# Four products of two heads' weighted sums side by side in a fixed order: the grouped layers of a hybrid decoder trunk

## The chip, the cores and the metric

The kernel runs on one core of one Trainium2 chip. The metric is the device time of one execution in microseconds (us), lower is better. The kernel before takes 2571.69 us, the median of 3 runs between 2570.69 and 2571.88.

## What is computed

The reference is a trunk of four decoder layers for 256 rows of 2048 features in fp32. Layers 0 and 3 are latent attention, layer 1 is sparse attention with a top-k selection, layer 2 is attention in a window of 128 keys. Every layer also has four heads that attend to a memory, a gate over all head outputs, and an output projection. Layers 1 and 2 have 32 query heads of 64 features that share 4 key and value heads. The part that the change touches is the last line of their attention, the weighted sum of the values. Layer 2, cut to what matters (layer 1 differs in which keys a query may see, and has no sink):

```python
def block(args):
    qb, kb, vb, start = args
    ...
    s = jnp.einsum('bqgjd,bkgd->bgjqk', qb, kb, preferred_element_type=jnp.float32) * scale + bias
    s = jnp.where(valid, s, NEG_INF)
    m = jnp.maximum(jnp.max(s, axis=-1, keepdims=True), sink)
    e = jnp.exp(s - m)
    p = e / (jnp.sum(e, axis=-1, keepdims=True) + jnp.exp(sink - m))
    return jnp.einsum('bgjqk,bkgd->bqgjd', p.astype(vb.dtype), vb)
...
y = jnp.concatenate([self_out, mem_out], axis=-1) * jax.nn.silu(gate)
x = x + y @ w_out[i]
```

## The kernel before

**Projections.** All weights stream from DRAM through one ring of buffers (`wr`). ScalarE copies each piece of 128x512 into a rounded part `wh` (L74), VectorE takes the remainder `wl` (L83), and TensorE multiplies both parts with activations that are split in the same way. `rows_by` (its matmuls are L289) gives rows, `columns_by` (L310 for `wh`, L314 for `wl`) gives columns. These make up most of TensorE's work. `wh` and `wl` have three buffers each, so ScalarE waits where TensorE has not yet let go of one.

**A grouped layer.** `Grouped.project(g)` makes the queries of one key head `g` (eight query heads, as two halves of four), a bias tile and the gate tile `gT`. `Grouped.attend` then goes through the two halves. In each half it treats two sets, `odd` 0 and 1. A set holds two heads, and its 64 queries of one of four quarters stand as 128 columns. For each set `quarter_softmax` goes over the two halves `b` of the rows: score products (`sp`, L1033 and L1036), bias, minimum and exponential on VectorE and ScalarE, division by the sum, and `weights_T`, which transposes the weights on TensorE into a PSUM tile `ptp` (L550), two transposes for `b = 0` and four for `b = 1`. ScalarE copies the result into `pT[odd]` (L1061, recorded under the copy helper's line L74). The text calls the two sets the even and the odd head.

**The sums.** When both sets have their weights, four fp32 matrix products form the tile `o` in one PSUM bank (L1065). `v` is the stationary side, 128 keys by 64 features; the weights `pT` are the moving side. The even set's sums go to the partitions 0 to 63, the odd one's to 64 to 127, by the `tile_position`, which names the half of the array's columns. The first key tile (`t = 0`) streams 512 columns of weights, the second one (`t = 1`) only 256, as the first two quarters of the queries come before all of its keys. In the source the order is even and odd for `t = 0`, then even and odd for `t = 1`. Afterwards VectorE multiplies `o` with the gate (L1070) and the result is split into the two parts of `y`, which the output projection takes (L289, `acc_wo`).

**What sets the order.** The kernel is written for a framework whose planner decides the order of the instructions on each engine: it plays the program through with a model of times, and picks what it takes to be ready. An instruction may thus stand far from its place in the source, as long as what it depends on comes first. Writes to one PSUM tile keep their source order. `keep_in_program_order` pins one instruction: it adds an edge to the instruction that was traced just before it on the same engine, which sets an order of issue and is no wait for an end. It says nothing about what the planner puts between the two. The order of `project`, `attend` and the output projection of the part before (`w_out`) in the source is that of the loop over parts; the planner lets their matmuls run among the score and sum products of `attend`.

Of the kernel before, what the change touches and what calls it, by code (L numbers as in the profile page):

```python
# [16 lines left out]
S = 256  # L17
# [28 lines left out]
def kernel(ctx: ExitStack, tc: tile.TileContext, a: dict, out: bass.AP,  # L46
                             kinds=(0, 1, 2, 0)):
    nc = tc.nc
# [8 lines left out]
    def misc(name, dt=F32):  # L57
        return ps.tile([P, 512], dt, name=name, tag="mp", bufs=4)

    def tmp(name, n=512, dt=F32):  # L60
        return wk.tile([P, n], dt, name=name, tag=f"t{n}", bufs=4)
# [11 lines left out]
    def copy_act(o, i, scale=1.0):  # L73
        inst = nc.scalar.activation(o, i, AF.Copy, scale=scale)  # L74
        if pinned:
            tc.keep_in_program_order(inst)
# [4 lines left out]
    def split(hi, lo, src):  # L81
        copy_act(hi, src)
        nc.vector.tensor_sub(lo, src, f32(hi))  # L83
# [175 lines left out]
    def other_work():  # L259
        for _ in range(2):  # L260
            if steps and next(steps[0], None) is None:
                steps.pop(0)
# [294 lines left out]
    def attend(o, v, pT):  # L557

        for n_, (l, r_) in enumerate(((v[0], pT[0]), (v[0], pT[1]), (v[1], pT[0]))):
            nc.tensor.matmul(o, l, r_, start=n_ == 0, stop=False)  # L560
        nc.tensor.matmul(o[:, P:], v[2], pT[2], start=False, stop=True)
# [24 lines left out]
    def quarter_softmax(score, bias, first_key, both, b, nsk):  # L586

        es = []
        mn, sm = small("mn", 2), small("sm", 2)
        for i, r in enumerate((2 * b, 2 * b + 1)):  # L590
            k0, k1 = first_key(r), (r + 1) * 64
            n = k1 - k0
            sp = score(r, k0, n)
            u = wk.tile([P, S], F32, name="u", tag="e", bufs=4)
            e = wk.tile([P, S], F32, name="e", tag="e", bufs=4) if nsk is None else u
            for z0, z1 in ((0, k0), (k1, (b + 1) * P)):
                if z0 < z1:
                    nc.gpsimd.memset(e[:, z0:z1], 0.0)
            bi, at = bias(r, k0, k1), u[:, k0:k1]
            if both(r):  # L600
                nc.vector.tensor_add(at, sp[:, n:2 * n], bi)
                bi = at
            nc.vector.tensor_tensor_reduce(at, sp[:, :n], bi, -1.0, nsk if nsk is not None else BIG,
                                           op0=OP.add, op1=OP.min, accum_out=mn[:, i:i + 1])
            nc.scalar.activation(e[:, k0:k1], at, AF.Exp, bias=mn[:, i:i + 1], scale=-1.0,
                                 accum_out=sm[:, i:i + 1])
            es.append((e, k0, k1))
        rc = small("rc", 2)
        if nsk is not None:
            d = small("sd", 2)  # L610
            nc.vector.tensor_scalar(d, mn, nsk, None, op0=OP.subtract)
            e2 = small("se", 2)
            nc.scalar.activation(e2, d, AF.Exp)
            s3 = small("sa", 2)
            nc.vector.tensor_add(s3, sm, e2)
            nc.vector.reciprocal(rc, s3)
        else:
            nc.vector.reciprocal(rc, sm)
        for i, (e, k0, k1) in enumerate(es):
            copy_act(e[:, k0:k1], e[:, k0:k1], scale=rc[:, i:i + 1])  # L620
        return weights_T([e for e, _, _ in es], [(i, k) for k in range(b + 1) for i in range(2)])
# [82 lines left out]
    class Latent:  # L704
# [121 lines left out]
        def attend(self, qn, qr, kn, v, gT):  # L826
            y = act.tile([P, 2, 4, S], F32R, name="y", tag="y", bufs=2)
            for h in range(4):
                def score(b):
                    sp = misc("sp")  # L830
                    qs = slice(b * P, (b + 1) * P)
                    q, k, z = qn[h // 2], kn[h // 2], h % 2
                    if b == 0:
                        seq = [(q[:, 0, z, qs], k[:, :, z, :P]), (q[:, 1, z, qs], k[:, :, z, :P]),
                               (qr[:, h, qs], self.kr[:, :, :P])]
                    else:
                        seq = [(q[:, 0, z, qs], k[:, :, z, :]), (q[:, 1, z, qs], k[:, 0, z, :]),
                               (qr[:, h, qs], self.kr)]
                    for n_, (l, r_) in enumerate(seq):
                        n = r_.shape[-1] * (r_.shape[1] if len(r_.shape) == 3 else 1)  # L840
                        nc.tensor.matmul(sp[:, :n], l, r_, start=n_ == 0, stop=n_ == 2)
                    return sp
                tp = masked_softmax(score, lambda b, n: caus[:, S - n:], self.scale)
                pT = wk.tile([P, 768], F32R, name="pT", tag="pT", bufs=PT)
                pT = pT[:, :S], pT[:, S:2 * S], tmp("pf")[:, :P]
                split(pT[0], pT[1], tp[:, :S])
                copy_act(pT[2], tp[:, S:S + P])
                if h % 2 == 0:
                    o = misc("o")
                attend(o[:, (h % 2) * S:(h % 2 + 1) * S],  # L850
                       [z[:, h * P:(h + 1) * P] for z in v], pT)
                if h % 2 == 1:
                    gated(y, o, gT, h - 1)
            return y


    class Grouped:
# [164 lines left out]
        def attend(self, g, q, bm, gT):  # L1022
            while steps:
                other_work()
            y = act.tile([P, 2, 4, S], F32R, name="y", tag="y", bufs=2)
            for half in range(2):
                pT = []
                for odd in range(2):
                    def score(r, k0, n):
                        sp = misc("sp")  # L1030
                        qb = q[half][:, odd, r].rearrange("p j c -> p (j c)")
                        if both(r):
                            nc.tensor.matmul(sp[:, :2 * n], qb, self.k[:, g, :, k0:k0 + n], start=True, stop=True)  # L1033
                        else:
                            for v in range(2):
                                nc.tensor.matmul(sp[:, :n], qb, self.k[:, g, v, k0:k0 + n],  # L1036
                                                 start=v == 0, stop=v == 1)
                        return sp

                    def bias(r, k0, k1):  # L1040
                        c0 = (3 - r) * 64
                        bh = bm[:, half * 2 + odd, c0 + k0:c0 + k1]
                        if not self.sparse or r == 0:
                            return bh
                        bs = wk.tile([P, S], F32, name="bs", tag="e", bufs=4)[:, :k1]
                        nc.vector.tensor_add(bs, bh, self.sel[r])
                        return bs

                    def first_key(r):
                        return 64 if r == 3 and not self.sparse else 0  # L1050

                    def both(r):
                        return r < 3 or not self.sparse

                    u0 = g * 4 + half * 2 + odd
                    nsk = None if self.sparse else nsink[:, u0:u0 + 1]
                    pT.append(wk.tile([P, 6, P], F32, name="pT2", tag="pT", bufs=PT))
                    for b in range(2):
                        tp = quarter_softmax(score, bias, first_key, both, b, nsk)
                        i0, i1 = ((0, 2), (2, 6))[b]  # L1060
                        copy_act(pT[odd][:, i0:i1], tp[:, :(i1 - i0) * P].rearrange("p (i c) -> p i c", c=P))  # L1061
                o = misc("o")
                for t in range(2):
                    for odd in range(2):
                        nc.tensor.matmul(o[64 * odd:64 * odd + 64, t * S:], self.v[:, t, g * 64:g * 64 + 64],  # L1065
                                         pT[odd][:, 4 * t:4 + 2 * t].rearrange("p i c -> p (i c)"),
                                         start=t == 0, stop=t == 1, tile_position=(0, 64 * odd))
                j = half * 2
                yt = tmp("yt")
                nc.vector.tensor_mul(yt.rearrange("p (j r c) -> p j r c", j=2, r=4),  # L1070
                                     o.rearrange("p (r j c) -> p j r c", r=4, j=2),
                                     gT[:, j:j + 2, :].rearrange("p j (r c) -> p j r c", r=4))
                split(y[:, 0, j:j + 2, :], y[:, 1, j:j + 2, :], yt.rearrange("p (a b) -> p a b", a=2))
            return y
# [237 lines left out]
```

## Time and profile before

| what | value |
|---|---|
| median of 3 runs | 2571.69 us (2570.69 to 2571.88) |
| the profiled execution's own time | 2570.63 us |
| its span, first to last instruction | 2568.9 us |
| granted TensorE clock, mean | 0.999 |
| TensorE matmul busy | 2558.5 us |
| VectorE busy | 1885.3 us |
| ScalarE busy | 1596.3 us |
| DMA, mean over the span | 199 GB/s |

A row of the timeline gives the start and the length in us, the engine, the line, the operation, the tile that is written and those that are read, the shapes, and after `x` how many instructions of one kind in succession are merged in the row. PE is TensorE; PEld is its weight load, which can run beside a matmul. A row of the groups gives the count after `x`, then the busy time of all together, the mean length in ns, and the idle time before them. A row of the waits names who waited for whom, then the total in us, how often, and the longest. A matmul's recorded length overlaps with the next ones, so the step from one start to the next says more of its price than its length.

### The profile page before, as it was taken

The page shows a single profiled execution, that of the slowest core. Times are in us where ns is not written, and L with a number is a line of the kernel's source. Part 1 is how long each engine was busy: PE and PEld are TensorE (multiplying, and loading weights), DVE is VectorE, ACT ScalarE, POOL GpSimd, SP SyncE. Part 2 cuts the span into 40 slices and gives each one's busy share as a digit, 9 for nine tenths or more (in the row PEclk, how much of TensorE's full clock was granted, in tenths as well). Part 3 has the DMA queues.
Part 4 walks back from the last instruction along what each step waited for, and adds up shares of the span by engine and source line. Part 5 has one row for each costly group of instructions (what it writes and reads, how often), then busy time and mean ns, then how long its engine had stood idle before and what let it go on. Part 6 is the DMA issues. An engine that isn't in the chain of part 4 may idle for free.

```text
span 2568.9 us, 41673 instructions
## 1 busy us (share of the span) xinstructions
PE 2558.5 (100%) x14022; PEld 2186.3 (85%) x14022; DVE 1885.3 (73%) x3800; ACT 1596.3 (62%) x3271; POOL 102.9 (4%) x297
## 2 busy tenths in 40 slices
PE   9999999999999999999999999999999999999998
PEld 8888898888888889888888888888888888888887
DVE  6666667677777687987777777777768767777766
ACT  6556556566566566666666566666656666666655
POOL 1200000000000000000000000000000000000000
PEclk9999999999999999999999999999999999999999
DMA  9888777576677667665666565565555768666765
GB/s 310 262 265 257 238 224 227 165 196 178 183 203 204 185 199 205 197 194 164 185 181 175 170 214 179 165 180 166 176 168 161 238 189 221 190 195 186 222 168 185
DMA packets 478583, 511.68 MB, mean 199 GB/s; under 512 B 70656, under 2 KB 391040, under 8 KB 477728
## 3 DMA queue, kind: packets, MB, share of 16 engines
q1 hardware_dynamic: 461856, 451.82, 59.9%
q0 software_dynamic: 15792, 56.22, 7.0%
q8 instruction: 110, 1.80, 0.3%
q14 instruction: 105, 0.86, 0.1%
q10 hardware_dynamic: 720, 0.98, 0.1%
HBM read 483.67 MB, written 29.46 MB: 200 GB/s over the span
## 4 chain that ended last, share of the span: by engine, by line
PE 98%; DMA 1%; DVE 1%; ACT 0%; issue 0%; SPq 0%; POOL 0%; ACTq 0%; DVEq 0%
PE acc_wo L289 20%; PE acc_g L310 14%; PE acc_g L314 7%; PE acc_mv L289 7%; PE acc_q L310 5%; PE acc_mk L310 5%; PE acc_mq L310 4%; PE acc_cq L310 3%; PE acc_qn L310 3%; PE acc_q L314 2%; PE acc_mk L314 2%; PE acc_mq L314 2%; PE acc_cq L314 2%; PE acc_qr L310 2%; PE acc_qn L314 2%; PE acc_va L289 2%
## 5 line engine op out<-in xcount | busy, mean ns | idle before, releaser
L83 DVE TENSOR_TENSOR wl<-wr,wh 128x512 fp32r<-128x512 f32 (+1 forms) x1712 | 1154.5, 679 | 581.1 <-ACT wh L74 551.5
L74 ACT ACTIVATE wh<-wr 128x512 fp32r<-128x512 f32 (+1 forms) x1712 | 1063.0, 623 | 830.9 <-PE acc_g L310 148.1
L310 PE MATMUL acc_g<-xT,wh 128*128 128x512 f32 x1536 | 483.4, 397 | 0.0
L289 PE MATMUL acc_wo<-wh,y 128*128 128x512 f32 x1504 | 477.1, 392 | 0.0
L289 PEld LDWEIGHTS acc_wo<-wh,y 128*128 128x128 f32 x1504 | 282.5, 188 | 58.9 <-ACT th L531 1.5
L314 PEld LDWEIGHTS acc_g<-xT,wl 128*128 128x128 f32 x1536 | 280.8, 188 | 60.6 <-DVE wl L83 0.5
L314 PE MATMUL acc_g<-xT,wl 128*128 128x256 f32 x1536 | 306.0, 281 | 0.1
L289 PE MATMUL acc_wo<-wl,y 128*128 128x512 f32 x752 | 297.7, 396 | 0.0
L310 PEld LDWEIGHTS acc_g<-xT,wh 128*128 128x128 f32 x1536 | 235.3, 189 | 0.8
L289 PEld LDWEIGHTS acc_wo<-wl,y 128*128 128x128 f32 x752 | 141.4, 188 | 25.9
L310 PE MATMUL acc_q<-xT,wh 128*128 128x512 f32 x512 | 161.3, 396 | 0.0
L310 PE MATMUL acc_mq<-xT,wh 128*128 128x512 f32 x512 | 161.1, 396 | 0.0
L310 PE MATMUL acc_mk<-mT,wh 128*128 128x512 f32 x512 | 160.7, 395 | 0.0
L289 PE MATMUL acc_mv<-wh,mT 128*128 128x512 f32 x512 | 156.8, 390 | 0.2
L310 PE MATMUL acc_qn<-cT,wh 128*128 128x512 f32 x384 | 121.0, 396 | 0.0
L310 PE MATMUL acc_cq<-xT,wh 128*128 128x512 f32 x384 | 120.9, 396 | 0.0
L1231 DVE TENSOR_TENSOR xc<-xc,acc_wo 128x1024 f32<-128x1024 f32 x92 | 112.0, 1218 | 4.2 <-PE acc_wo L289 3.4
L314 PEld LDWEIGHTS acc_mk<-mT,wl 128*128 128x128 f32 x512 | 95.8, 188 | 22.6 <-DVE wl L83 0.2
L289 PEld LDWEIGHTS acc_mv<-wh,mT 128*128 128x128 f32 x512 | 96.3, 188 | 20.7 <-ACT wh L74 0.9
L314 PEld LDWEIGHTS acc_q<-xT,wl 128*128 128x128 f32 x512 | 95.0, 188 | 21.5
L314 PEld LDWEIGHTS acc_mq<-xT,wl 128*128 128x128 f32 x512 | 94.5, 188 | 21.4 <-issue 0.4
L314 PE MATMUL acc_mq<-xT,wl 128*128 128x256 f32 x512 | 101.8, 280 | 0.0
(325 smaller groups left out, 3837.1 us busy)
## 6 DMA issues: line engine op xcount, KB each, us to landing
wr<-in_w_out_dram SPq DMA_DIRECT2D x188, 512.0 KB, 3.7
wr<-in_w_in_a_dram SPq DMA_DIRECT2D x176, 512.0 KB, 4.2
wr<-in_w_mem_kv_dram SPq DMA_DIRECT2D x126, 512.0 KB, 4.8
wr<-in_w_in_b_dram SPq DMA_DIRECT2D x116, 512.0 KB, 3.6
wr<-in_w_in_c_dram SPq DMA_DIRECT2D x104, 512.0 KB, 3.5
wr<-in_w_uq_dram SPq DMA_DIRECT2D x288, 128.0 KB, 2.8
wr<-in_w_in_a_dram SPq DMA_DIRECT2D x32, 288.0 KB, 3.1
mv<-mv POOLq DMA_DIRECT2D x16, 512.0 KB, 6.5
```

The source lines that it names most:

```text
L74: inst = nc.scalar.activation(o, i, AF.Copy, scale=scale)
L83: nc.vector.tensor_sub(lo, src, f32(hi))
L289: nc.tensor.matmul(acc[t][:, :n], q[:, v, (s + k) % 4, t * P:(t + 1) * P], w_[:, :n], start=s + k == 0 and v == 0 and w_ is wh, stop=s + k ...
L310: nc.tensor.matmul(acc[j], wh[:, o:o + P], q[:, :, kt % 4, :], start=kt == 0, stop=False)
L314: nc.tensor.matmul(acc[j][:, 0, :], wl[:, o:o + P], q[:, 0, kt % 4, :], start=False, stop=kt == kts - 1)
L1231: nc.vector.tensor_add(xs, xs, acc)
```

## The change

The two nested loops keep their products; only the order of the inner loop turns, and each product is pinned behind the matmul that was traced before it. For the first of the four that is the last transpose of the odd set's weights.

```diff
                 o = misc("o")
                 for t in range(2):
-                    for odd in range(2):
-                        nc.tensor.matmul(o[64 * odd:64 * odd + 64, t * S:], self.v[:, t, g * 64:g * 64 + 64],
-                                         pT[odd][:, 4 * t:4 + 2 * t].rearrange("p i c -> p (i c)"),
-                                         start=t == 0, stop=t == 1, tile_position=(0, 64 * odd))
+                    for odd in (1, 0):
+                        tc.keep_in_program_order(
+                            nc.tensor.matmul(o[64 * odd:64 * odd + 64, t * S:], self.v[:, t, g * 64:g * 64 + 64],
+                                             pT[odd][:, 4 * t:4 + 2 * t].rearrange("p i c -> p (i c)"),
+                                             start=t == 0, stop=t == 1, tile_position=(0, 64 * odd)))
```

## The prediction

> **What bounds the kernel now.** I read the page's busy times first, then the chain that ended last, then the waits, and then the timeline of TensorE around the changed line, where every term of the sum comes from.
>
> ```profile
> span 2568.9 us, 41673 instructions
> PE 2558.5 (100%) x14022; PEld 2186.3 (85%) x14022; DVE 1885.3 (73%) x3800; ACT 1596.3 (62%) x3271; POOL 102.9 (4%) x297
> ...
> PE 98%; DMA 1%; DVE 1%; ACT 0%; issue 0%; SPq 0%; POOL 0%; ACTq 0%; DVEq 0%
> ```
>
> TensorE is busy for 2558.5 of 2568.9 us, and 98% of the chain is its own instructions, one behind another. VectorE has a quarter of the span free, ScalarE over a third. The waits say the same from the other side:
>
> ```profile
> PE wu L122 <- DVE ones L116: 1.1, 1, 1.1
> PE msp L663 <- DMA mkr<-mkT: 0.6, 1, 0.6
> ...
> ACT wh L74 <- PE acc_g L310: 148.1, 223, 2.1
> ```
>
> The first two rows are all that TensorE waited for another engine: 1.7 us. The third is ScalarE, which splits the weights, waiting 148.1 us for TensorE to give a weight buffer back. So the makers of the weights stand behind TensorE, and what is taken from TensorE's stream should come off the time. Only the two grouped layers contain the changed line. There are 16 groups of products (2 layers, 4 key heads, 2 halves), and the question is what each group takes out of TensorE's stream. Its row in the groups, and the two shapes kept apart:
>
> ```profile
> L1065 PE MATMUL o<-pT,vs 128*64 128x256 f32 (+1 forms) x128 | 41.2, 505 | 0.0
> ...
> L1065 PE MATMUL o<-pT,vs 128*64 128x512 f32 x64 | 34.3, 618 | 0.0
> L1065 PE MATMUL o<-pT,vs 128*64 128x256 f32 x64 | 19.8, 392 | 0.0
> ```
>
> 64 and 64 for 16 groups: each group has four matrix products, and each product is recorded as two passes. The two products of the first key tile stream 512 columns, those of the second 256 (they skip the queries that this tile cannot reach). The means of 618 and 392 ns can't simply be added, since passes lie beside each other. So I go by the distance from start to start in the timeline. A group of the first half (TensorE only):
>
> ```profile
> 1123.22 0.27 PE L550 MATMUL ptp<-ident,e 128*128 128x128 f32 x1
> 1123.42 1.07 PE L1065 MATMUL o<-pT,vs 128*64 128x512 f32 x2
> 1124.42 0.50 PE L1033 MATMUL sp<-kd,qS 128*128 128x128 f32 x2
> 1124.76 0.49 PE L550 MATMUL ptp<-ident,e 128*128 128x128 f32 x3
> 1125.01 0.36 PE L314 MATMUL acc_g<-xT,wl 128*128 128x256 f32 x1
> ...
> 1128.30 0.39 PE L289 MATMUL acc_wo<-wl,y 128*128 128x512 f32 x1
> 1128.53 0.39 PE L289 MATMUL acc_wo<-wh,y 128*128 128x512 f32 x1
> 1128.84 1.50 PE L1065 MATMUL o<-pT,vs 128*64 128x512 f32 x6
> 1130.28 0.50 PE L289 MATMUL acc_wo<-wh,y 128*128 128x512 f32 x1
> 1130.62 0.40 PE L289 MATMUL acc_wo<-wl,y 128*128 128x512 f32 x1
> ```
>
> and the last group of all, which is of the second half:
>
> ```profile
> 1879.59 0.27 PE L550 MATMUL ptp<-ident,u 128*128 128x128 f32 x1
> 1879.79 1.07 PE L1065 MATMUL o<-pT,vs 128*64 128x512 f32 x2
> 1880.79 0.55 PE L550 MATMUL ptp<-ident,u 128*128 128x128 f32 x3
> 1881.09 0.49 PE L314 MATMUL acc_mq<-xT,wl 128*128 128x256 f32 x2
> ...
> 1885.24 1.50 PE L1065 MATMUL o<-pT,vs 128*64 128x512 f32 x6
> 1886.67 0.39 PE L314 MATMUL acc_mq<-xT,wl 128*128 128x256 f32 x1
> ```
>
> The even head's 512-column product (two passes) runs **alone**, in the middle of the odd head's transposes. The other three products come about 5.4 us later as one block of six passes. All 16 groups have this form, 8 like the first and 8 like the last. The lone product takes 1124.42 - 1123.42 = 1.00 us of TensorE. The block of three products takes 1130.28 - 1128.84 = 1.44 us although it streams twice as many columns (2 x (512 + 256 + 256) against 2 x 512). Inside the block:
>
> ```profile
> 1128.84:1128.85 0.01, 0.01 (x1) 0.01 (x2) 1.00 0.00 0
> 1128.85:1129.11 0.26, 0.26 (x2) 0.19 (x4) 1.00 0.00 0
> ```
>
> These are stretches of that line alone (length, TensorE busy, passes in flight, weight loads busy, clock, DMA). From 1128.85 on two passes are in flight, at most 0.01 us apart, at a clock of 1.00. Two narrow windows of the timeline show single passes later in the block:
>
> ```profile
> 1129.32 0.59 PE L1065 MATMUL o<-pT,vs 128*64 128x512 f32 x1
> ...
> 1129.97 0.38 PE L1065 MATMUL o<-pT,vs 128*64 128x256 f32 x1
> ```
>
> The first is the odd 512-column product's second pass, which starts 0.48 us after its first; the other is the last pass, of the odd 256-column product. The even head's 256-column product, which writes the other 64 partitions of the sum, lies wholly beside the odd head's 512-column one and costs nothing.
>
> **The change, part by part.** No instruction is added or taken away. The source order becomes odd first tile, even first tile, odd second, even second, and each is pinned behind the matmul traced before it. The odd head's first product stands behind that head's last transpose, so the even head's first product, now pinned behind it, can't be issued early any more.
>
> Removed: the lone product from its place. Its price is the sequence with it against the same sequence without it, which the trace has for other heads:
>
> ```profile
> 1087.06 0.60 PE L550 MATMUL ptp<-ident,e 128*128 128x128 f32 x4
> 1087.41 0.48 PE L314 MATMUL acc_q<-xT,wl 128*128 128x256 f32 x2
> ...
> 1110.74 0.27 PE L550 MATMUL ptp<-ident,e 128*128 128x128 f32 x1
> 1110.77 0.48 PE L1033 MATMUL sp<-kd,qS 128*128 128x128 f32 x2
> 1111.09 0.49 PE L550 MATMUL ptp<-ident,e 128*128 128x128 f32 x3
> 1111.34 0.48 PE L314 MATMUL acc_g<-xT,wl 128*128 128x256 f32 x2
> ```
>
> Second half: four transposes up to the next weight matmul take 1087.41 - 1087.06 = 0.35 us. With the product among them they take 1881.09 - 1879.59 = 1.50. The place costs 1.15 us: 1.00 for the product and 0.15 for what the neighbours lose at its edges. First half: transpose, two score products, three transposes take 1111.34 - 1110.74 = 0.60 us, with the product 1125.01 - 1123.22 = 1.79, so 1.19. Over the groups: 8 x 1.15 + 8 x 1.19 = 18.7 us.
>
> Added: the even 512-column product in the block. The trace doesn't show two 512-column products side by side, so it has two bounds. From below it is the stagger, 0.01 us: as in the block of before, the even product lies beside the odd one. The two second-tile products then lie beside each other where the odd one now runs alone, and the block stays at 0.48 + 0.43 + 0.22 + 0.22 + 0.09 = 1.44 us (the steps between the starts above, each pass as long as its columns, and the exit). It could not be less, as the odd head's four passes set it. From above the product is not overlapped at all: two passes, 0.48 + 0.43 = 0.91 us. I take 0.01, because for the 256 columns that overlap in the rows of before the odd product's passes keep exactly the step (0.48) that the lone product's have, so a second stream beside them slowed nothing. For 16 groups: 0.2 us.
>
> The wait. The block waits for ScalarE's copy of the odd head's weights out of PSUM, as its odd product does now:
>
> ```profile
> 1125.29 0.60 ACT L74 ACTIVATE pT<-ptp 128x512 f32<-128x512 f32 x1 [1.93 <-PE ptp L550]
> ```
>
> It ends at 1125.89, 2.95 us before the block starts; this stretch lies behind the lone product and loses no cover with it. Behind the block on TensorE's queue stand the output projection's and the next weight matmuls, and VectorE's gating product (L1070) waits for it, as before. No DMA is issued or moved and SP and POOL are passed by nothing. The PSUM bank of the sums is taken 5.4 us later, which only frees it for the scores. What is late next: the weight splits must come 18.7 us earlier in sum between 1123 and 1887 us, 2%, against a quarter idle on VectorE.
>
> Sum: 18.7 - 0.2 = 18.5 us. The profiled execution took 2570.63 us (1.7 outside its span), 1.06 below the median of 2571.69. 2570.63 - 18.5 = 2552.1, as a median **2553.2 us**. The planner lays out all instructions anew from its own model. I allow 3 us either way for that: a change of shape costs about 0.1 us (1128.53 to 1128.84 is 0.31 us where the step before it is 0.23), and two more or fewer per group make 16 x 0.2.
>
> **A rule that speaks against it.** In the rows above the even head's pass starts by 1128.85, ahead of the odd head's second pass at 1129.32, though its product stands behind the odd one in the source. So passes of the two column halves do not wait for each other's turn there. Were starts to keep the source order, the even first pass would begin at 0.49 in the block and its second at 0.92, the odd second-tile passes at 0.93 and 1.15, and the even ones at 1.35 and 1.57: the block ends at 1.88, 0.44 longer, 7.0 us in all, and the time is 2553.2 + 7.0, about 2560. The Trainium skill, page "TensorE: Matmul & The Clock Gate", Part 3, section "The mechanism", states just this rule: matmuls start and end in program order, strictly first in, first out, while tiles in different positions start about 4 ns apart. The trace agrees with the small stagger and, at the level of passes, not with the strict order.
>
> **The rivals.**
> - *Two pairs instead of four* (other matmuls planned between the first and the second tile's products; a pin holds only the order). The pair of 512 then costs what the lone product costs now (1.17 us, the mean of 1.15 and 1.19). Today's block with its edges takes 0.08 (entry, 0.31 - 0.23) + 1.44 + 0.11 (the 0.34 after it, less 0.23) = 1.63. The pair of 256 takes 0.08 + 0.27 + 0.22 + 0.09 + 0.11 = 0.77, where the 0.27 is a 256-column pass with the 0.05 by which a block's first pass is longer (0.48 against 0.43). A group saves 0.86, together 13.8: 2558. Against it: today's three stand together in the groups shown, though the planner was free to part them.
> - *Strict order*, above: 2560.
> - *No overlap*: 16 x (1.17 - 0.91) = 4.2 us saved, 2567.5.
> - *The cover goes* (slower). The planner could set the block right behind the transposes, since it counts four products there. TensorE then stands from 1125.01 to the copy's end at 1125.89, 0.9 us, and that nearly eats the 1.17: 2567. If a weight split (0.6 us on ScalarE, as the copy) goes ahead of the copy, it stands 1.5 us and the kernel becomes slower by 16 x 0.33 = 5.3 us, 2577. It decides from a wait of 1.17 us on. Against it: the block's start has 2.95 us of cover, and the planner knows the wait.
> - *Nothing comes off*, because another engine sets the pace: 2571.7. Against it speaks ScalarE's wait for TensorE.
>
> **How the numbers follow.** A measurement of this kernel can tell about 0.2%, 5.1 us, from no change. The forecast has 0.77, two pairs 0.07, strict order 0.06, no overlap 0.02, the cover gone without loss 0.03, with loss 0.03, another pace 0.02. Faster by over 0.2% (below 2566.5): 0.77 + 0.07 + 0.06 = 0.90. Within: 0.02 + 0.03 + 0.02 = 0.07. Slower: 0.03. The range takes the forecast with its 3 us and reaches to the strict order with some: 2549.5 to 2562.
>
> **What would show it.** Right: no `o<-pT,vs` row of two passes alone; 16 blocks of eight passes, each about 1.44 us from its start to the next matmul, with two 512-column passes in flight from the first 0.01 us; odd transposes that again take 0.35 us or 0.60 to the next weight matmul; the busy time of L1065 down from 41.2 us (its row in the groups) to about 25; no new TensorE wait. Wrong: a block near 1.9 or 2.3 us (order or no overlap), or idle TensorE ahead of L1065 released by the copy `pT<-ptp`. The forecast falls if L1065 shrinks as said and the span does not.

## The result, and the profile after

The changed kernel takes 2555.85 us (median of 6 runs, 2554.03 to 2556.82), the kernel before 2571.28 in the same runs (6 runs, 2570.51 to 2571.88). The ratio is 0.994 with a 95% interval of 0.9927 to 0.9952. That is 15.4 us faster, where the forecast was 18.5 (2553.2). The profiled execution took 2556.82 us.

The page of the kernel after, its first lines and the chain:

```profile
span 2555.0 us, 41674 instructions
PE 2541.7 (99%) x14022; PEld 2184.8 (86%) x14022; DVE 1882.8 (74%) x3800; ACT 1597.1 (63%) x3271; POOL 103.6 (4%) x297
...
PE 98%; DMA 1%; DVE 0%; ACT 0%; issue 0%; SPq 0%; POOL 0%; DVEq 0%
```

Each of these engines has as many instructions as before, and TensorE is still the chain. The products' line (now L1066) in the groups, merged and then by shape:

```profile
L1066 PE MATMUL o<-pT,vs 128*64 128x512 f32 (+1 forms) x128 | 24.2, 498 | 0.0
...
L1066 PE MATMUL o<-pT,vs 128*64 128x512 f32 x64 | 17.3, 618 | 0.0
...
L1066 PE MATMUL o<-pT,vs 128*64 128x256 f32 x64 | 9.6, 379 | 0.0
```

It covers 24.2 us of TensorE in place of 41.2, with the same passes of the same mean length (618 ns at 512 columns). They lie beside each other now. The first block, in TensorE's timeline:

```profile
1123.92 0.60 PE L550 MATMUL ptp<-ident,e 128*128 128x128 f32 x4
1124.27 0.48 PE L314 MATMUL acc_g<-xT,wl 128*128 128x256 f32 x2
...
1128.13 1.51 PE L1066 MATMUL o<-pT,vs 128*64 128x512 f32 x8
1129.57 0.50 PE L1033 MATMUL sp<-kd,qS 128*128 128x128 f32 x2
...
1203.19 1.51 PE L1066 MATMUL o<-pT,vs 128*64 128x512 f32 x8
```

The four transposes are together again and take 0.35 us to the next weight matmul. The block has eight passes and takes 1129.57 - 1128.13 = 1.44 us, as forecast. The last row is the same place one key head (two groups) later, 75.06 us on. In the kernel before the block that follows the one at 1128.84 in this way is

```profile
1206.24 1.50 PE L1065 MATMUL o<-pT,vs 128*64 128x512 f32 x6
```

77.40 us on. So a key head gives 2.34 us and a group 1.17, the forecast's mean. The inside of the block (stretches of that line alone; the passes in flight stand in brackets behind TensorE's busy time):

```profile
1128.12:1128.14 0.02, 0.01 (x2) 0.02 (x2) 1.00 0.03 0
1128.14:1128.60 0.46, 0.46 (x2) 0.18 (x4) 1.00 0.13 36
1128.62:1129.03 0.41, 0.41 (x4) 0.13 (x2) 1.00 0.00 0
```

Two passes of 512 columns start within 0.02 us of each other. The first two rows show only these two in flight. The third counts four: the two second passes, and the ends of the first two, which are recorded beyond the start of the next.

Not all is as forecast, however. TensorE has waits that it did not have before:

```profile
PE acc_g L310 <- DVE mqT L352: 1.9, 1, 1.9
PE msp L663 <- DMA mkr<-mkT: 1.3, 1, 1.3
PE wu L122 <- DVE ones L116: 1.1, 1, 1.1
PE acc_mv L289 <- ACT wh L74: 0.8, 2, 0.5
```

The second was 0.6 us before and differs from run to run (0.6 in the sixth experiment's profile, 1.6 in the fifth's). The fourth stands in the first 14 us, far ahead of the changed lines, and differs as well (0.2 in the third's, 1.3 in the fifth's). The first did not exist before. It stands at the end of layer 2's attention, behind the last block:

```profile
1873.23 1.51 PE L1066 MATMUL o<-pT,vs 128*64 128x512 f32 x8
1874.67 0.74 PE L663 MATMUL msp<-mkr,mqT 128*128 128x256 f32 x4
1877.33 1.22 PE L310 MATMUL acc_g<-xT,wh 128*128 128x512 f32 x2 [1.92 <-DVE mqT L352]
...
1880.80 0.39 PE L314 MATMUL acc_g<-xT,wl 128*128 128x256 f32 x2
1881.03 0.63 PE L310 MATMUL acc_g<-xT,wh 128*128 128x512 f32 x2
...
1881.74 0.63 PE L310 MATMUL acc_g<-xT,wh 128*128 128x512 f32 x2
```

The gate's first matmul needs an accumulator, and both hold memory queries that VectorE has not emptied. VectorE's own timeline tells why:

```profile
1873.78 0.69 DVE L83 TENSOR_TENSOR wl<-wr,wh 128x512 fp32r<-128x512 f32 x1 [0.71 <-ACT wh L74]
1874.79 0.69 DVE L1071 TENSOR_TENSOR yt<-o,gT 128x512 f32<-128x512 f32 x1 [0.33 <-PE o L1066]
1875.40 1.28 DVE L351 TENSOR_TENSOR zl<-acc_mq,mqT 128x512 f32<-128x512 f32 x2
1876.60 0.68 DVE L352 TENSOR_TENSOR mqT<-zl,acc_mq 128x512 fp32r<-128x512 f32 x1
```

The two subtractions that empty the accumulators (L351) stand behind the gating product (L1071), which waits for the block. The kernel before has the same order on VectorE:

```profile
1886.78 0.69 DVE L1070 TENSOR_TENSOR yt<-o,gT 128x512 f32<-128x512 f32 x1 [1.58 <-PE o L1065]
1887.39 0.68 DVE L351 TENSOR_TENSOR zl<-acc_mq,mqT 128x512 f32<-128x512 f32 x1
```

But there TensorE still had matmuls of the memory queries (`acc_mq`) to do behind the block, from 1886.67 to 1891.67, and did not wait. In the change the planner has put all of these ahead of the block, and only the score products of 0.74 us are left to cover the emptying. The stretches over all engines (the clock is the number before the last two) show a second price:

```profile
1872.00:1875.40 3.40, 3.40 (x20) 1.99 (x18) 1.99 (x3) 1.45 (x3) 0.00 (x0) 1.00 0.60 183
1875.40:1877.30 1.90, 0.01 (x1) 0.00 (x0) 1.90 (x5) 0.63 (x1) 0.00 (x0) 0.98 0.34 119
1877.30:1880.30 3.00, 2.97 (x9) 2.59 (x10) 1.17 (x2) 0.37 (x1) 0.00 (x0) 0.50 0.00 0
```

After the wait the granted clock is 0.50 for the 3 us of the last row (3.41 us in all, see the last section). From 1877.33 to 1880.80 TensorE takes 3.47 us for three pairs of `wh` and two pairs of `wl` matmuls. A little later, at full clock, a pair of each takes 0.71 us (1881.03 to 1881.74), of which the `wl` pair takes 0.23 (1880.80 to 1881.03). So the work is 2 x 0.71 + 0.48 = 1.90. The wait costs 1.9 us and the clock 1.6: 3.5 together.

The half clock does not come in every execution. Four kernels have this wait: the change and those of experiments 1, 3 and 6. Of their 23 executions, 13 show a mean granted clock of 0.998, among them the four whose traces show the half clock, and 10 show 0.999, as do all 70 executions of the other kernels in the experiments. For the change, three took 2556.32 to 2556.82 us (0.998) and three 2554.03 to 2555.38 (0.999). Their means lie 1.9 us apart, near the 1.6 of the half clock.

### The profile page after: what moved, and what is told of

It is laid out like the page before. It is cut to its first block, busy times and chain, and to the rows that moved or that the text cites. A ratio compares the mean times of both kernels' runs of the same rounds, so it can differ in the third digit from the quotient of the medians.

```text
span 2555.0 us, 41674 instructions
## 1 busy us (share of the span) xinstructions
PE 2541.7 (99%) x14022; PEld 2184.8 (86%) x14022; DVE 1882.8 (74%) x3800; ACT 1597.1 (63%) x3271; POOL 103.6 (4%) x297
## 4 chain that ended last, share of the span: by engine, by line
PE 98%; DMA 1%; DVE 0%; ACT 0%; issue 0%; SPq 0%; POOL 0%; DVEq 0%
PE acc_wo L289 20%; PE acc_g L310 14%; PE acc_g L314 7%; PE acc_mv L289 7%; PE acc_q L310 5%; PE acc_mk L310 5%; PE acc_mq L310 4%; PE acc_cq L310 4%; PE acc_qn L310 4%; PE acc_q L314 2%; PE acc_mk L314 2%; PE acc_mq L314 2%; PE acc_cq L314 2%; PE acc_qr L310 2%; PE acc_qn L314 2%; PE acc_va L289 2%
## 5 line engine op out<-in xcount | busy, mean ns | idle before, releaser
L83 DVE TENSOR_TENSOR wl<-wr,wh 128x512 fp32r<-128x512 f32 (+1 forms) x1712 | 1155.0, 679 | 582.3 <-ACT wh L74 549.9
L314 PEld LDWEIGHTS acc_g<-xT,wl 128*128 128x128 f32 x1536 | 282.0, 188 | 61.5 <-DVE wl L83 0.5
L314 PE MATMUL acc_g<-xT,wl 128*128 128x256 f32 x1536 | 306.1, 281 | 0.0
L314 PEld LDWEIGHTS acc_mk<-mT,wl 128*128 128x128 f32 x512 | 95.8, 188 | 22.6 <-DVE wl L83 0.2
L314 PEld LDWEIGHTS acc_q<-xT,wl 128*128 128x128 f32 x512 | 94.7, 188 | 21.5 <-issue 0.4
L314 PEld LDWEIGHTS acc_mq<-xT,wl 128*128 128x128 f32 x512 | 94.5, 188 | 21.2
L314 PE MATMUL acc_q<-xT,wl 128*128 128x256 f32 x512 | 102.0, 281 | 0.0
```

Of the source, the lines that this page charges most:

```text
L314: nc.tensor.matmul(acc[j][:, 0, :], wl[:, o:o + P], q[:, 0, kt % 4, :], start=False, stop=kt == kts - 1)
```

## The experiments

Times are medians. The kernel before took 2571.39 us in the runs beside the first four and 2571.31 beside the last four. The code is cut, with `...` for what is left out, and shown against the kernel after. Where the order is turned, the edit writes the two loops as one and pins on a line of its own.

**1. The order without the pins.** The change's order, nothing pinned:

```diff
-                for t in range(2):
-                    for odd in (1, 0):
-                        tc.keep_in_program_order(
...
+                for t, odd in ((0, 1), (0, 0), (1, 1), (1, 0)):
...
+                    if False:
+                        tc.keep_in_program_order(mm)
```

> Odd first as in the change, but none of the four products is pinned. Theory A: what keeps the even head's first product back is only its place behind the odd one among the writes to the one tile o, and the planner holds that order with or without a pin; then 16 blocks of eight passes stand as in the change and the time is the change's, 2555.9 us within 1.5. Theory B (as the prediction put it): the pins hold it back; without them a product runs alone again and the time is that of before, 2571.3 us.

It took 2554.73 us (2553.66 to 2556.11), ratio 0.9936 (0.9923 to 0.995). The planner's order is the change's on every engine, instruction for instruction: 16 blocks of eight. Theory A holds. The odd-first order alone makes the change, and the pins add nothing. The 1.1 us to the change's median are the scatter of one program, whose executions reach from 2553.66 to 2556.82 us in the two runs.

**2. The pins without the order.** All four pinned, even first:

```diff
-                for t in range(2):
-                    for odd in (1, 0):
...
+                for t, odd in ((0, 0), (0, 1), (1, 0), (1, 1)):
...
+                    if True:
+                        tc.keep_in_program_order(mm)
```

> All four pinned, but even first as before. Theory A: the even head's first product may again be issued as soon as its pin lets it, behind the odd head's four transposes, three microseconds ahead of the odd head's copy; it stands alone and costs its 1.00 us and about 0.16 at the edges, now between weight matmuls; 16 blocks of six passes remain; the time is that of before within 2 us, 2571.3 (2569 to 2573). Theory B: pinning is what sets the four side by side, and the time is the change's, 2555.9 us.

It took 2571.76 us (2570.9 to 2572.95), ratio 1.0002 (0.9993 to 1.0011). The first group in TensorE's timeline:

```profile
1123.54 0.60 PE L550 MATMUL ptp<-ident,e 128*128 128x128 f32 x4
1124.07 1.07 PE L1064 MATMUL o<-pT,vs 128*64 128x512 f32 x2
1125.07 0.50 PE L314 MATMUL acc_g<-xT,wl 128*128 128x256 f32 x2
...
1128.73 1.50 PE L1064 MATMUL o<-pT,vs 128*64 128x512 f32 x6
```

The lone product has moved behind the transposes and costs the same there: 1.00 us itself, and its edges. Theory A holds. A pin sets an order of issue; it does not set two instructions side by side.

**3. How far ahead the second column half is taken up.** The block of the change, both odd products first, then both even ones:

```diff
-                for t in range(2):
-                    for odd in (1, 0):
...
+                for t, odd in ((0, 1), (1, 1), (0, 0), (1, 0)):
...
+                    if True:
+                        tc.keep_in_program_order(mm)
```

> The four stand in one block as in the change, but in the order odd first tile, odd second tile, even first tile, even second tile, so that the even head's products stand two places behind. Theory A (passes of the two column halves are taken up independently, however far behind they stand): the block still takes 1.44 us and the time is the change's, 2555.9. Theory C (only the next product is looked at): the even head's first pass starts with the odd head's second product, at 0.91 us, and the block takes about 2.35 us; 16 x 0.91 = 14.6 us more, 2570.4. Theory D (passes start in source order): the even head starts at 1.13 us, the block takes about 2.5 us, 16 x 1.08 = 17.3 more, 2573.

It took 2556.93 us (2554.41 to 2557.37), ratio 0.9941 (0.9926 to 0.9957), the change's time. The first block's stretches, and its place in the timeline:

```profile
1127.91:1127.92 0.01, 0.01 (x1) 0.01 (x1) 1.00 0.00 0
1127.93:1128.39 0.46, 0.46 (x2) 0.19 (x4) 1.00 0.15 45
```

```profile
1127.91 1.52 PE L1064 MATMUL o<-pT,vs 128*64 128x512 f32 x8
1129.36 0.50 PE L1033 MATMUL sp<-kd,qS 128*128 128x128 f32 x2
```

A second pass is in flight from 1127.93 on, although the even head's first product now stands two places behind (the trace names no head; that the order of issue is the edit's rests on the pins). The block takes 1129.36 - 1127.91 = 1.45 us. Theories C (2.35) and D (2.5) are out. The two column halves take their passes up independently, over at least one product in between.

**4. The remainder's buffer moved.** The change, and in the helper that empties an accumulator:

```diff
-        z = tmp("zl").rearrange("p (j c) -> p j c", j=2)
+        z = part_tile(F32)[:].rearrange("p (j c) -> p j c", j=2)
```

> The change, and the remainder of a split head (zl) takes its buffer from another pair of buffers of the same size, which is free at that time, instead of the four that it shares with the gated product yt. Theory A: the change's new wait of TensorE at 1875 us comes from VectorE emptying the first of the two accumulators of the memory queries only behind the gating of the last block, as there is no buffer free for it; with its own buffer it comes ahead, the gate's matmuls start before the last block, the wait of 1.9 us and the half clock behind it (together about 3.9 us) are gone, and the time is 2552.0 us. Theory E: the wait lies in the order that the block itself forces and stays: 2555.9 us.

It took 2552.92 us (2552.76 to 2554.03), ratio 0.993 (0.9917 to 0.9942). The end of layer 2 on TensorE, then on VectorE:

```profile
1870.99 0.63 PE L310 MATMUL acc_g<-xT,wh 128*128 128x512 f32 x2
...
1872.94 1.51 PE L1066 MATMUL o<-pT,vs 128*64 128x512 f32 x8
1874.38 0.50 PE L314 MATMUL acc_g<-xT,wl 128*128 128x256 f32 x2
```

```profile
1860.04 0.68 DVE L351 TENSOR_TENSOR hl<-acc_mq,mqT 128x512 f32<-128x512 f32 x1
1861.43 0.68 DVE L352 TENSOR_TENSOR mqT<-hl,acc_mq 128x512 fp32r<-128x512 f32 x1
```

The first accumulator is emptied at 1860 to 1862, 15 us earlier, the gate's matmuls start ahead of the last block, and the wait is gone. Theory A holds for the mechanism. The gain is 2.9 us over the change's median, or 1.8 over the same program in the first experiment (whose fastest run, 2553.66, lies among these), where 3.9 was expected. The 3.9 counted the half clock in full, but only three of the change's six executions have it by their mean clock. And 0.5 us went to a wait for a weight split in layer 3 (in TensorE's waits `acc_qn L314 <- DVE wl L83`). It goes with the other buffer, as the eighth experiment has 0.3 of it without the change. This version is the fastest of all that ran, 18.5 us below the kernel before.

**5. and 6. Each layer by itself.** The change in the sparse layer alone (the diff), and in the window layer alone (`if not self.sparse`). The other layer has the old order, unpinned:

```diff
-                for t in range(2):
-                    for odd in (1, 0):
...
+                for t, odd in (((0, 1), (0, 0), (1, 1), (1, 0)) if self.sparse else ((0, 0), (0, 1), (1, 0), (1, 1))):
...
+                    if self.sparse:
+                        tc.keep_in_program_order(mm)
```

> The change in the sparse layer (layer 1) alone, eight groups; layer 2 is in the old order. Theory A: a group gives 1.17 to 1.19 us and layer 1 keeps all of it, as its profile shows no new wait: 2571.4 - 9.4 = 2562.0 us. Theory F: each of the 16 groups gives an equal 0.97 us (15.4 / 16), less than the lone product's place: 2571.4 - 7.7 = 2563.7.

> The change in the window layer (layer 2) alone. Theory A: its eight groups give 9.4 us and the new wait at the layer's end with the half clock behind it takes 3.9 back: 2571.4 - 5.5 = 2565.9 us, and the wait of the gate's matmul for VectorE stands in the profile. Theory F: 2571.4 - 7.7 = 2563.7.

The sparse layer took 2561.76 us (2560.7 to 2562.9), ratio 0.9963 (0.9949 to 0.9976), a gain of 9.55. The window layer took 2565.06 (2563.91 to 2566.75), ratio 0.9977 (0.9967 to 0.9986), a gain of 6.25. The wait is in the profile of the window layer's run:

```profile
PE acc_g L310 <- DVE mqT L352: 1.9, 1, 1.9
```

Theory A fits both: full gain in layer 1, and in layer 2 the gain less some 3 us. An equal share (7.7 each) fits neither median, though its 2563.7 lies within 0.3 us of the second one's fastest run.

**7. The gated product's buffer moved instead.** The change, and `yt` of the grouped layers from the other pair of buffers:

```diff
-                yt = tmp("yt")
+                yt = part_tile(F32)[:]
```

> The change, and now the gated product yt has the other pair of buffers, while the remainder of a split head stays with the four shared ones. Theory A (the shared buffers alone put the emptying of the accumulator behind the gating): as with the remainder moved, the wait at the end of layer 2 is gone, 2552.9 us. Theory E (moving the remainder helped in some other way): the wait stays, 2555.9 us.

It took 2555.72 us (2555.39 to 2555.99), ratio 0.9939 (0.9927 to 0.9952). The time is theory E's, but the wait at the layer's end is gone, as A said. Another came:

```profile
PE acc_g L310 <- DVE hl L999: 2.8, 2, 1.4
```

Two waits of 1.4 us, both in layer 2, where the gate waits for an accumulator that holds query heads. Their work tile (L999) lives in that same pair of buffers, which `yt` now takes. So the pair was not free for `yt`. The time is 2.8 us above the fourth experiment's, as much as these two waits. It says nothing on the shared buffers; that the first wait went does.

**8. The buffer alone.** The kernel before with the fourth experiment's edit:

> The kernel before, with the remainder of a split head in the other pair of buffers, without the change. Theory A: there was no wait of TensorE to remove, so nothing changes: 2571.4 us within 1. Theory G: the other buffers speed up this kernel by themselves, as much as they did on top of the change: 2571.4 - 2.9 = 2568.5 us.

It took 2571.86 us (2570.25 to 2572.85), ratio 1.0002 (0.9993 to 1.0011). Theory A holds: the other buffer gains nothing where nothing waits.

## Why the prediction was right, and where it was off

**The place of the lone product** (18.7 us): right. The step from one key head to the next gives 1.17 us a group, and the sparse layer by itself gives 9.55 for its eight (8 x 1.17 = 9.4).

**The even product in the block** (0.01 us): right. A second 512-column stream beside the first slowed nothing; the block is 1.44 us, and 1.45 in the turned order.

**Why it can't be issued early**: the step failed in its cause. The prediction said that the even head's first product, "now pinned behind" the odd one, can't be issued early any more. The pins do nothing here. Without them the planner makes the same program, and with them in the old order the lone product stays. What is left to hold it back is the order of the writes to the one tile `o`, which the planner keeps as in the source. The odd product is last ready, and it now comes first. This is by exclusion: no run put the two heads' sums into two tiles.

**What is late next**: this step failed, and the missing 3.1 us are there. It looked at weight splits alone, and the prediction's sign "no new TensorE wait" did not hold. What came late was the emptying of an accumulator, planned behind the gating of the last block in layer 2. It stood there in the kernel before too, but TensorE then had other matmuls behind the block; in the new layout it has 0.74 us of them. By the profile the wait costs 1.9 us and the half clock behind it 1.6, together 3.5. From 16 x 1.17 = 18.7 that leaves 15.2 with the half clock and 16.8 without it. The three executions at 0.998 gain 14.6 us in the mean and the three at 0.999 gain 16.5; the median, 15.4, lies between. For the two profiled executions, whose spans lie 13.9 us apart, the other two new waits (0.7 us more for the DMA and 0.8) close the sum: 15.2 - 1.5 = 13.7. With the remainder in another buffer the wait is gone and the time is 2552.92, within 0.3 us of the forecast. The 3 us allowed for the planner's new layout were large enough, but they were counted for changes of shape and not for a wait. That they took in this wait as well is luck.

**The rivals.** Strict order of the passes (2560) and no overlap (2567.5) are out by the block's length, two pairs (2558) by the 16 blocks of eight. Its slower rival, a wait for ScalarE's copy ahead of the block, did not come. The wait that did come is of the same family: TensorE has too little work to cover what it needs next. But it stands behind the block and not ahead of it, and what is late is on VectorE's queue. The rule of the Trainium skill that was weighed, matmuls in strict program order (page "TensorE: Matmul & The Clock Gate", Part 3, "The mechanism"), fits these traces in the stagger alone: in the third experiment the pass of a product two places behind starts 0.02 us after the first.

## What to carry to other kernels

Of products that share the array by column halves and whose order the planner keeps, put those that are ready last first in the source. Here none then went alone, and the second half's products cost 0.01 us a group. When a block moves, look on every engine's queue at what is planned behind its consumer, above all what empties accumulators, and at how much work the bounding engine has left to cover it. Temporaries that share a few buffers tie such work together.

## What was not expected of the hardware

In the change a TensorE wait of 1.92 us was followed by half the granted clock, and so was the same wait in the other three runs that have it (the first, the third and the window layer's). Waits of 1.6 us (the sparse layer's run, at 1514.7, for a DMA) and of 1.4 us (the seventh run, at 1724) were not followed by any.

The clock records of the traces say when the clock changes. In the four runs with the wait at the end of layer 2, the half clock behind it lasts 3.41 us each time. The stretch at full clock ahead of it lasts 1870.50 us in three of them and 1880.74 in the window layer's run, 548 and 551 times that length. So the clock changes on a grid of 3.41 us here. Along this grid, the stretch with the wait and the one behind it (TensorE only; its busy time, the clock, then the DMA), for the change, the window layer's, the sparse layer's and the seventh run:

```profile
1873.82:1877.23 3.41, 1.59 (x12) 1.00 0.51 154
1877.24:1880.65 3.41, 3.32 (x10) 0.50 0.00 0
```

```profile
1882.88:1886.28 3.40, 1.48 (x10) 1.00 0.38 131
1886.29:1889.70 3.41, 3.41 (x12) 0.50 0.00 0
```

```profile
1513.77:1517.17 3.40, 1.77 (x12) 1.00 1.10 386
1517.18:1520.59 3.41, 3.41 (x24) 1.00 0.85 290
```

```profile
1723.98:1727.39 3.41, 2.02 (x13) 1.00 0.47 147
1727.40:1730.80 3.40, 3.40 (x21) 1.00 0.09 21
```

Half clock came behind a busy share of 0.47 (1.59 of 3.41) and less, 0.43 and 0.44 in the third and the first experiment's traces. None came behind 0.52 (1.77 of 3.40) and more, and from the first clock record to TensorE's last matmul no other stretch of the ten traces lies below that. So these traces fit a clock that goes by TensorE's busy share on the grid, with a border between 0.47 and 0.52. A wait of 1.63 us (the sparse layer's) alone leaves 0.52 in its stretch; one of 1.92 leaves 0.44 if the grid does not part it, and more if it does. That would explain why only some executions have the half clock, as the grid lies elsewhere in each trace (its first border is 0.2 to 3.3 us behind the first instruction). It is not shown, since no trace was kept of an execution with this wait and without the half clock.

The Trainium skill, page "TensorE: Matmul & The Clock Gate", section "Why this matters for your kernels", asks for no idle gap beyond about 3 us; here 1.92 was enough in the traces kept. Whether the half-array passes that ran just ahead of the wait count for less was not tried and stays open.
